# Two halves of an activation, one matmul of 512 columns: the first feed-forward product of a two-layer encoder

## The chip, the cores and the metric

The kernel runs on one core of a Trainium2 chip. The metric is the device time of one execution in microseconds (us), shown as the median of the runs of a kernel. TensorE is called PE here, its loading of a stationary operand PEld, VectorE DVE, ScalarE ACT, GpSimd POOL and SyncE SP.

## What is computed

The reference is a trunk of two layers over 256 tokens of width 1024. In each layer four token mixers are gated and summed, and then comes the feed-forward part, which the change touches:

```
def rms_norm(x, g):
    y = x * lax.rsqrt(jnp.mean(x * x, axis=-1, keepdims=True) + NORM_EPS)
    return y * g

def hybrid_layer(x, ...):
    ...
    x = x + jnp.sum(gates * proj, axis=2) @ w_o
    hf = rms_norm(x, g_ffn)
    x = x + jnp.square(jax.nn.relu(hf @ w_up)) @ w_down     # w_up 1024 x 4096, w_down 4096 x 1024
    return x
```

All data are fp32. One layer follows the other, and a last `rms_norm` closes the trunk.

## The kernel before, in words

**Products in halves.** PE is given operands of the type fp32r. Every fp32 operand is kept as two such tensors, a high half (its cast) and a low half (what the cast leaves over), and a product is the sum of three matmuls: high by high, high by low and low by high. The helper `mm3` (L122 to L124) issues them into one PSUM tile. The operand that is loaded into PE is the stationary one; the other one streams past it column by column. Each matmul brings its own load of the stationary operand, also where two matmuls in a row use the same one.

**Weights.** `weights` (L103) fetches a 128 x 1024 tile by a DMA issued on SP (L110), casts it to the high half `hi` on ACT (L114) and takes the rest `lo` on DVE (L115). There are 5 buffers for `raw` and 4 each for `hi` and `lo`, so the cast of a tile waits until PE has let go of the tile four before it.

**The first product.** `w_up` comes in 32 tiles of 128 hidden units. For one tile, `mtile` runs over the 8 blocks `k` of the model width: stationary is the block of the weight, and the 256 columns (tokens) of the activation `xg2` move past it, so 24 matmuls of 256 columns fill half of a PSUM tile `pu` of 512 columns. The high and the low half of `xg2` are two tiles, `xgh` and `xgl`, which `scale_split` writes on ACT (L293) and DVE (L294).

**On the way out of PSUM.** `hidden` (L797) makes the squared ReLU and its two halves:

```
nc.scalar.activation(r, ps[:, :T], AF.Relu)                                            # L801
nc.vector.scalar_tensor_tensor(t, ps[:, :T], 0.0, r, op0=ALU.max, op1=ALU.mult)        # L802
nc.scalar.copy(hi, t)                                                                  # L803, into U
nc.vector.tensor_tensor(lo, t, hi, op=ALU.subtract)                                    # L804, into U
```

**The second product.** `second` takes one hidden tile as the stationary operand and lets 512 columns of `w_dn` move past it: 12 matmuls of 512 columns for a tile, into four PSUM tiles `pd` that gather over all 32 hidden tiles.

**The order of the work.** The order on PE is that of the program. For the other engines a scheduler sets the order when the kernel is built, and an engine keeps to it at run time: an instruction that waits holds up all that stand behind it. In the loop over `i`, a step is the first product of tile `i` followed by the second product of tile `i - 2` (`LAG` is 2). It begins with a block of three tiles (`EARLY`): their first four `k`, the transposes of the other half of the activation, their last four `k`, and then at once the second product of tile 0, which needs `hidden` of tile 0. From `i = 3` on the loop runs in pairs, 29 steps to a layer.

Of the kernel before, what the change touches and what calls it, by code (L numbers as in the profile page):

```python
# [15 lines left out]
F32R = mybir.dt.float32r  # L19
I32 = mybir.dt.int32  # L20
AF = mybir.ActivationFunctionType
ALU = mybir.AluOpType
AX = mybir.AxisListType.X

P = 128
T = 256
D = 1024
KT = D // P
# [42 lines left out]
def hybrid_trunk(ctx: ExitStack, tc: tile.TileContext, xT, xtok, pos, small, gfin, abias, w_lat, w_v, w_in, w_uq, w_ukv,  # L71
                 w_gate, w_br, w_o, w_up, w_dn, out):
    nc = tc.nc
# [5 lines left out]
    act = ctx.enter_context(tc.tile_pool(name="act", bufs=1))  # L79
# [10 lines left out]
    def nm(s):  # L90
        count[0] += 1
        return f"{s}_{count[0]}"
# [9 lines left out]
    def weights(src, n=WCOLS, pieces=1, between=None):  # L102
        raw = rawp.tile([P, WCOLS], F32, tag="raw", name=nm("raw"))  # L103
        hi = whp.tile([P, WCOLS], F32R, tag="hi", name=nm("hi"))
        lo = wlp.tile([P, WCOLS], F32R, tag="lo", name=nm("lo"))
        share[0] += 1
        eng = nc.gpsimd if share[1] and share[0] % share[1] == 0 else nc.vector
        w = n // pieces
        for c in range(0, n, w):
            nc.sync.dma_start(raw[:, c:c + w], src[:, c:c + w])  # L110
            if c == 0 and between is not None:
                between()
        for c in range(0, n, w):
            cut = nc.scalar.copy(hi[:, c:c + w], raw[:, c:c + w])  # L114
            done = eng.tensor_tensor(lo[:, c:c + w], raw[:, c:c + w], hi[:, c:c + w], op=ALU.subtract)  # L115
        if eng is nc.vector:
            share[2] = done
        return hi, lo, done, cut

    def mm3(ps, stat, mov, first, last, late_mov=False):  # L120
        (sh, sl), (mh, ml) = stat[:2], mov[:2]
        nc.tensor.matmul(ps, sh, mh, start=first, stop=False)  # L122
        nc.tensor.matmul(ps, *((sl, mh) if late_mov else (sh, ml)), start=False, stop=False)  # L123
        nc.tensor.matmul(ps, *((sh, ml) if late_mov else (sl, mh)), start=False, stop=last)  # L124

    def cols(pair, i):
        return pair[0][:, i * P:(i + 1) * P], pair[1][:, i * P:(i + 1) * P]

    def part(pair, i):
        return pair[0][:, i, :], pair[1][:, i, :]  # L130
# [151 lines left out]
        return rb  # L282

    def new_xg():
        return (act.tile([P, KT, T], F32R, tag="xgh", name=nm("xgh")),
                act.tile([P, KT, T], F32R, tag="xgl", name=nm("xgl")))

    def scale_split(xg, k, src, g, on_vector=False):

# [6 lines left out]
    def to_features(half, dst, gcol, pool, tag):  # L296

        for pr in range(2):
            pt = pool.tile([P, 512], F32, tag=tag, name=nm("pt"))
            for j in range(2):  # L300
                k = 4 * half + 2 * pr + j
                for b in range(NB):
                    nc.tensor.transpose(pt[:, j * T + b * P:j * T + (b + 1) * P], X[:, b, k * P:(k + 1) * P], ident)
            for j in range(2):
                k = 4 * half + 2 * pr + j
                scale_split(dst, k, pt[:, j * T:(j + 1) * T], gcol(k))
# [9 lines left out]
    for _ in range(WARM):  # L316
        nc.tensor.matmul(warm[:, 0:P], o256, o256, start=True, stop=True)

    xg = new_xg()
    acc2 = tmp.tile([P, 2, T], F32, tag="d1", name="acc2", bufs=1)  # L320
    total = acc2[:, 0, :]
# [3 lines left out]
    for l in range(L):  # L325
# [7 lines left out]
        def tick():  # L333
            if side:
                for f in side.pop(0):
                    f()
# [4 lines left out]
        def mtile(ps, src, rhs, pieces=1):  # L341
            w = weights(src, pieces=pieces)
            for k in range(KT):
                mm3(ps, cols(w, k), part(rhs, k), k == 0, k == KT - 1)
            tick()
# [4 lines left out]
        for g in range(KT // 2):  # L350
            def stream(k0, k1):
                nc.sync.dma_start(xin[:, k0:k1, :], xT[:, k0:k1, :])
                for k in range(k0, k1):
                    scale_split(xg, k, xin[:, k, :], col(C_GMIX + k), on_vector=k % 2 == 1)

            if l == 0 and g == 0:
                stream(0, 1)
                w = weights(w_lat[l, g], 2 * LAT, pieces=2, between=lambda: stream(1, 2))
            else:
                if l == 0:  # L360
                    stream(2 * g, 2 * g + 2)
                w = weights(w_lat[l, g], 2 * LAT, pieces=1 if l else 2)
# [4 lines left out]
            for j in range(2):  # L367
                k, o = 2 * g + j, j * LAT
# [40 lines left out]
        for b in range(NB):  # L409
            nc.vector.scalar_tensor_tensor(z[:, b, :], plat[b][:, 384:388], rc[:, b:b + 1], s[:, C_BF:C_BF + HEADS],  # L410
                                           op0=ALU.mult, op1=ALU.add)
# [240 lines left out]
        def mla():  # L652
            w = weights(w_uq[l])
            for pr in range(2):
                ps = new_ps("puq")
                for e in range(2):
                    h = 2 * pr + e
                    for k in range(2):
                        mm3(ps[:, e * T:(e + 1) * T], cols(w, 2 * h + k), part(lat, k), k == 0, k == 1)
                nc.vector.tensor_tensor(qB[:, 2 * pr:2 * pr + 2, :], ps2(ps), CS, op=ALU.mult)  # L660
            w = weights(w_ukv[l], 512)
            for pr in range(2):
                ps = new_ps("puk")
                mm3(ps[:, :T], cols(w, pr), part(lat, 2), True, True)
                nc.scalar.copy(kB[0:64, 2 * pr, :], ps[0:64, :T])
                nc.scalar.copy(kB[64:P, 2 * pr + 1, :], ps[64:P, :T])
            ps = new_ps("puv")
            for b in range(NB):
                st = (lat[0][:, 2, b * P:(b + 1) * P], lat[1][:, 2, b * P:(b + 1) * P])
                mm3(ps[:, b * 256:(b + 1) * 256], st, (w[0][:, 256:512], w[1][:, 256:512]), True, True)  # L670
            nc.scalar.copy(VB.rearrange("p b d -> p (b d)"), ps)
            tick()
# [92 lines left out]
        def block(pair, k, b):  # L765
            return pair[0][:, k, b * P:(b + 1) * P], pair[1][:, k, b * P:(b + 1) * P]

        xg2 = new_xg()
        po = {(b, h): new_ps("po") for h in range(2) for b in range(NB)}

# [8 lines left out]
        for kp, h in ((0, 0), (0, 1), (1, 0), (1, 1), (2, 0), (2, 1), (3, 0), (3, 1)):  # L779
            w = weights(w_o[l, kp, h])  # L780
            for b in range(NB):
                for j in range(2):
                    k = 2 * kp + j
# [13 lines left out]
        def hidden(i, ps):  # L797
            t = tmp.tile([P, T], F32, tag="ut", name=nm("ut"))
            r = tmp.tile([P, T], F32, tag="sq", name=nm("ur"))
            hi, lo = U[:, i % RING, 0, :], U[:, i % RING, 1, :]  # L800
            nc.scalar.activation(r, ps[:, :T], AF.Relu)  # L801
            nc.vector.scalar_tensor_tensor(t, ps[:, :T], 0.0, r, op0=ALU.max, op1=ALU.mult)  # L802
            nc.scalar.copy(hi, t)  # L803
            nc.vector.tensor_tensor(lo, t, hi, op=ALU.subtract)  # L804

        def new_pu(i):
            pool, tag = ((psc, "sc"), (ppv, "pv"), (pms, "ms"), (pms, "ms"))[i % 4]
            return pool.tile([P, 512], F32, tag=tag, name=nm("pu"))

        EARLY = 3  # L810
        ws = [weights(w_up[l, i]) for i in range(EARLY)]
        pu = [new_pu(i) for i in range(EARLY)]
        for half in range(2):
            for i in range(EARLY):
                for k in range(4 * half, 4 * half + 4):
                    mm3(pu[i][:, :T], cols(ws[i], k), part(xg2, k), k == 0, k == KT - 1)
                if half == 0 and i == 0:
                    to_features(1, xg2, gffn, pmm, "mm")
        for i in range(EARLY):
            hidden(i, pu[i])  # L820
        pd = {(b, h): new_ps("pd") for b in range(NB) for h in range(2)}

        def second(i, w, b, h):
            st = U[:, i % RING, 0, b * P:(b + 1) * P], U[:, i % RING, 1, b * P:(b + 1) * P]
            tokens(pd[b, h], st, w, h, i == 0, i == FT - 1)
# [5 lines left out]
        last = []  # L831
        for i in range(FT + LAG):
            if EARLY <= i < FT:
                ps = new_pu(i)
                mtile(ps[:, :T], w_up[l, i], xg2)
                hidden(i, ps)
            d = i - LAG
            if d < 0:
                continue
            w = weights(w_dn[l, d])  # L840
            if d >= FT - 2:
                last.append((d, w))
                continue
            for b in range(NB):
                for h in range(2):
                    second(d, w, b, h)

        if l + 1 < L:
            xg = new_xg()
            s1 = sm[l + 1]  # L850

            def gmix(k):
                return s1[:, C_GMIX + k:C_GMIX + k + 1]

            for h in range(2):
                for b in range(NB):
                    for d, w in last:
                        second(d, w, b, h)
                    added(b, h)
                    if (h, b) == (1, 0):  # L860
                        to_features(0, xg, gmix, pms, "ms")
            stream_turn.append(lambda xg=xg, gmix=gmix: to_features(1, xg, gmix, pms, "ms"))
            continue
# [99 lines left out]
```

## Time and profile before

| what | value |
|---|---|
| runs | 844.81 us median (844.4 to 846.23, 3 runs) |
| the profiled execution, its own time | 843.17 us |
| its span in the trace | 841.4 us |
| PE busy | 823.5 us, 98% of the span |
| PEld busy | 757.9 us, 90% |
| DVE busy | 570.1 us, 68% |
| ACT busy | 449.5 us, 53% |
| POOL busy | 153.0 us, 18% |
| mean granted share of PE's clock | 0.998 |

The span reaches from the first to the last instruction of the program; the execution's own time is 1.8 us longer. Busy times of the engines overlap. The end of a matmul in the trace is a model, and matmuls overlap in it, so what one costs is read from the distance between the starts of two that follow each other, not from its duration.

### The profile page before, as it was taken

Reading aid. Unit: us, or ns where it says so; the run is one execution under the profiler, and the core shown is the slowest. Engines: PE = TensorE matmul, PEld = TensorE weight load, DVE = VectorE, ACT = ScalarE, POOL = GpSimd, SP = SyncE. Lnnn points to the kernel's source line nnn. Section 1 sums busy time; section 2 is a strip of 40 time slices with the busy share of each in tenths; the row PEclk is TensorE's granted clock in tenths of the full one; section 3 lists DMA queues with packets and bytes.
Section 4 is the critical chain, followed back from the end, with each engine's and each line's share of the span. In section 5 each row is a group of like instructions: output and inputs, shape, how many; then the busy total and the mean of one; then the engine's idle time right before and its main releaser. Section 6 shows DMA issues by size and latency. Waiting matters only on the chain.

```text
span 841.4 us, 14516 instructions
## 1 busy us (share of the span) xinstructions
PE 823.5 (98%) x5646; PEld 757.9 (90%) x5646; DVE 570.1 (68%) x948; ACT 449.5 (53%) x757; POOL 153.0 (18%) x156
## 2 busy tenths in 40 slices
PE   8999999999999999999999999999999999999996
PEld 7879999999889999999899899999998899999995
DVE  7899984787675555555578899557866655555554
ACT  6755546654464444444485664485445554545443
POOL 6534232133200000000014332312331000000000
PEclk9999999999999999999999999999999999999999
DMA  8765343455556555656554534345555555555531
GB/s 278 223 211 173 125 140 128 160 184 192 161 165 201 179 196 181 193 181 197 165 174 160 190 129 149 130 133 173 193 176 200 174 183 194 188 189 181 194 127 50
DMA packets 42549, 145.55 MB, mean 173 GB/s; under 512 B 5104, under 2 KB 7408, under 8 KB 42352
## 3 DMA queue, kind: packets, MB, share of 16 engines
q1 hardware_dynamic: 41904, 142.98, 52.7%
q10 hardware_dynamic: 576, 1.64, 0.6%
q8 instruction: 44, 0.72, 0.4%
q14 instruction: 25, 0.20, 0.1%
HBM read 143.55 MB, written 1.05 MB: 172 GB/s over the span
## 4 chain that ended last, share of the span: by engine, by line
PE 91%; DVE 5%; issue 2%; POOL 1%; DMA 1%; ACT 0%; SPq 0%; POOLq 0%; DVEq 0%; ACTq 0%
PE pgt L122 7%; PE pgt L123 7%; PE pgt L124 7%; PE pu L123 7%; PE pu L124 7%; PE pd L123 7%; PE pu L122 7%; PE pd L122 7%; PE pd L124 7%; PE S L555 2%; DVE lo L115 2%; PE pqk L122 2%; PE pPV L593 2%; PE pqk L123 2%; PE pqk L124 2%; PE po L122 2%
## 5 line engine op out<-in xcount | busy, mean ns | idle before, releaser
L115 DVE TENSOR_TENSOR lo<-raw,hi 128x1024 fp32r<-128x1024 f32 (+3 forms) x241 | 298.4, 1241 | 196.6 <-ACT hi L114 194.4
L114 ACT CAST hi<-raw 128x1024 fp32r<-128x1024 f32 (+2 forms) x273 | 278.4, 1024 | 266.9 <-issue 208.7
L122 PE MATMUL pgt<-xgh,hi 128*128 128x256 f32 x512 | 149.5, 292 | 0.0
L122 PE MATMUL pu<-xgh,hi 128*128 128x256 f32 x512 | 144.9, 283 | 0.7 <-ACT xgh L293 0.7
L123 PE MATMUL pu<-xgl,hi 128*128 128x256 f32 x512 | 145.1, 283 | 0.3
L124 PE MATMUL pu<-xgh,lo 128*128 128x256 f32 x512 | 144.9, 283 | 0.0
L123 PE MATMUL pgt<-xgl,hi 128*128 128x256 f32 x512 | 144.7, 283 | 0.0
L124 PE MATMUL pgt<-xgh,lo 128*128 128x256 f32 x512 | 144.7, 283 | 0.0
L123 PE MATMUL pd<-hi,u 128*128 128x512 f32 x256 | 100.5, 393 | 1.1 <-DVE u L804 1.1
L122 PEld LDWEIGHTS pu<-xgh,hi 128*128 128x128 f32 x512 | 98.0, 191 | 3.4 <-ACT xgh L293 1.1
L122 PE MATMUL pd<-hi,u 128*128 128x512 f32 x256 | 100.7, 393 | 0.4 <-ACT u L803 0.4
L123 PEld LDWEIGHTS pu<-xgl,hi 128*128 128x128 f32 x512 | 98.0, 191 | 3.0 <-DVE xgl L294 0.7
L124 PE MATMUL pd<-lo,u 128*128 128x512 f32 x256 | 99.6, 389 | 0.0
L122 PEld LDWEIGHTS pgt<-xgh,hi 128*128 128x128 f32 x512 | 97.9, 191 | 0.8 <-issue 0.3
L123 PEld LDWEIGHTS pgt<-xgl,hi 128*128 128x128 f32 x512 | 98.1, 192 | 0.4
L124 PEld LDWEIGHTS pu<-xgh,lo 128*128 128x128 f32 x512 | 98.0, 191 | 0.0
L124 PEld LDWEIGHTS pgt<-xgh,lo 128*128 128x128 f32 x512 | 97.9, 191 | 0.0
L115 POOL TENSOR_TENSOR lo<-raw,hi 128x1024 fp32r<-128x1024 f32 (+1 forms) x32 | 77.2, 2414 | 110.7 <-ACT hi L114 106.1
L491 DVE SCALAR_TENSOR_TENSOR cacc<-up,sm,cacc 128x256 f32<-128x256 f32 x120 | 77.4, 689 | 0.0
L124 PEld LDWEIGHTS pd<-lo,u 128*128 128x128 f32 x256 | 48.1, 188 | 10.4
L123 PEld LDWEIGHTS pd<-hi,u 128*128 128x128 f32 x256 | 48.3, 189 | 9.4 <-DVE u L804 1.7
L122 PEld LDWEIGHTS pd<-hi,u 128*128 128x128 f32 x256 | 48.3, 189 | 9.2 <-ACT u L803 0.8
(254 smaller groups left out, 1356.8 us busy)
## 6 DMA issues: line engine op xcount, KB each, us to landing
raw<-in_w_gate SPq DMA_DIRECT2D x64, 512.0 KB, 3.8
raw<-in_w_up SPq DMA_DIRECT2D x64, 512.0 KB, 4.1
raw<-in_w_dn SPq DMA_DIRECT2D x64, 512.0 KB, 3.9
raw<-in_w_in SPq DMA_DIRECT2D x23, 512.0 KB, 4.2
raw<-in_w_br SPq DMA_DIRECT2D x16, 512.0 KB, 3.6
raw<-in_w_o SPq DMA_DIRECT2D x16, 512.0 KB, 4.4
raw<-in_w_v SPq DMA_DIRECT2D x8, 512.0 KB, 4.3
raw<-in_w_lat SPq DMA_DIRECT2D x8, 210.0 KB, 4.9
```

Source lines behind the costliest of these rows:

```text
L114: cut = nc.scalar.copy(hi[:, c:c + w], raw[:, c:c + w])
L115: done = eng.tensor_tensor(lo[:, c:c + w], raw[:, c:c + w], hi[:, c:c + w], op=ALU.subtract)
L122: nc.tensor.matmul(ps, sh, mh, start=first, stop=False)
L123: nc.tensor.matmul(ps, *((sl, mh) if late_mov else (sh, ml)), start=False, stop=False)
L124: nc.tensor.matmul(ps, *((sh, ml) if late_mov else (sl, mh)), start=False, stop=last)
L491: ins = nc.vector.scalar_tensor_tensor(cacc[:, c, :], up[:, c, j:j + T], wcol, cacc[:, c, :], op0=ALU.mult, op1=ALU.add)
L555: nc.tensor.matmul(sl, q[:, b * P:(b + 1) * P], k[:, 0:n], start=True, stop=True)
L593: nc.tensor.matmul(po[o:o + 64, 0:T], v[:, 0, vo:vo + HD], pts[:, 0:T], start=True, stop=False)
```

## The change

The two halves of the activation become one tile `xg` of shape 128 x 8 x 2 x 256, in which the high and the low half of a block `k` lie side by side. `mm2` replaces `mm3` in the first product: one matmul moves all 512 columns (high and low half) past the high half of the weight, and a second one moves the 256 columns of the high half past the low half of the weight, onto the left half of the PSUM tile. The PSUM tile then holds two partial sums side by side, and `hidden` adds them: ACT copies the right half out, DVE adds the left half to it, and a second DVE instruction makes the squared ReLU from the sum. The other users of the activation see the same two views as before.

```
+    def mm2(ps, stat, mov, first, last):
+        (sh, sl), (mh, both) = stat[:2], mov
+        nc.tensor.matmul(ps, sh, both, start=first, stop=False)
+        nc.tensor.matmul(ps[:, 0:T], sl, mh, start=False, stop=last)
+    def both(three, i):
+        return three[0][:, i, :], three[2][:, i, :, :]
...
     def new_xg():
-        return (act.tile([P, KT, T], F32R, tag="xgh", name=nm("xgh")),
-                act.tile([P, KT, T], F32R, tag="xgl", name=nm("xgl")))
+        xg = act.tile([P, KT, 2, T], F32R, tag="xg", name=nm("xg"))
+        return xg[:, :, 0, :], xg[:, :, 1, :], xg
...
             hi, lo = U[:, i % RING, 0, :], U[:, i % RING, 1, :]
-            nc.scalar.activation(r, ps[:, :T], AF.Relu)
-            nc.vector.scalar_tensor_tensor(t, ps[:, :T], 0.0, r, op0=ALU.max, op1=ALU.mult)
+            nc.scalar.copy(t, ps[:, T:512])
+            nc.vector.tensor_tensor(r, ps[:, :T], t, op=ALU.add)
+            nc.vector.scalar_tensor_tensor(t, r, 0.0, r, op0=ALU.max, op1=ALU.mult)
             nc.scalar.copy(hi, t)
             nc.vector.tensor_tensor(lo, t, hi, op=ALU.subtract)
...
-                    mm3(pu[i][:, :T], cols(ws[i], k), part(xg2, k), k == 0, k == KT - 1)
+                    mm2(pu[i], cols(ws[i], k), both(xg2, k), k == 0, k == KT - 1)
...
-                mtile(ps[:, :T], w_up[l, i], xg2)
+                w = weights(w_up[l, i])
+                for k in range(KT):
+                    mm2(ps, cols(w, k), both(xg2, k), k == 0, k == KT - 1)
                 hidden(i, ps)
```

What the engines are given differs in these places and in no other. On PE, at the beginning of the first product of a layer (`pu` the PSUM tile, `hi` and `lo` the halves of the weight), it was:

```order
L122 MATMUL pu_2905<-xgh_2705,hi_2888 128x256
L123 MATMUL pu_2905<-xgl_2706,hi_2888 128x256
L124 MATMUL pu_2905<-xgh_2705,lo_2889 128x256
L122 MATMUL pu_2905<-xgh_2705,hi_2888 128x256
L123 MATMUL pu_2905<-xgl_2706,hi_2888 128x256
L124 MATMUL pu_2905<-xgh_2705,lo_2889 128x256
```

and it is now:

```order
L131 MATMUL pu_2903<-xg_2704,hi_2886 128x512
L132 MATMUL pu_2903<-xg_2704,lo_2887 128x256
L131 MATMUL pu_2903<-xg_2704,hi_2886 128x512
L132 MATMUL pu_2903<-xg_2704,lo_2887 128x256
L131 MATMUL pu_2903<-xg_2704,hi_2886 128x512
```

Of three matmuls two have become one of 512 columns; the 256 columns of L124 (now L132) stay. Over both layers 1024 matmuls of 256 columns with their 1024 weight loads give way to 512 of 512 columns with 512 loads.

On ACT, at the end of the block of three tiles of layer 0 (`hi` a cast of a weight, `ur` or `ut` what is read from `pu`, `u` the high half of a hidden tile), it was:

```order
L114 CAST hi_3040<-raw_3039 128x1024
L801 ACTIVATE ur_2999<-pu_2905 128x256
L114 CAST hi_3076<-raw_3075 128x1024
L801 ACTIVATE ur_3005<-pu_2906 128x256
L803 CAST u_2886<-ut_2998 128x256
L114 CAST hi_3095<-raw_3094 128x1024
L801 ACTIVATE ur_3011<-pu_2907 128x256
```

and it is now:

```order
L115 CAST hi_3017<-raw_3016 128x1024
L812 COPY ut_2972<-pu_2903 128x256
L115 CAST hi_3046<-raw_3045 128x1024
L812 COPY ut_2979<-pu_2904 128x256
L115 CAST hi_3065<-raw_3064 128x1024
L815 CAST u_2884<-ut_2972 128x256
L812 COPY ut_2986<-pu_2905 128x256
```

The cast `u` of hidden tile 0 has moved from the fifth place to the sixth, behind the third cast of a weight.

On DVE at the same place (`lo` the low half of a weight, `u` the low half of a hidden tile), it was:

```order
L115 TENSOR_TENSOR lo_3041<-raw_3039,hi_3040 128x1024
L802 SCALAR_TENSOR_TENSOR ut_2998<-pu_2905,ur_2999 128x256
L115 TENSOR_TENSOR lo_3077<-raw_3075,hi_3076 128x1024
L804 TENSOR_TENSOR u_2886<-ut_2998,u_2886 128x256
L802 SCALAR_TENSOR_TENSOR ut_3004<-pu_2906,ur_3005 128x256
```

and it is now:

```order
L116 TENSOR_TENSOR lo_3018<-raw_3016,hi_3017 128x1024
L813 TENSOR_TENSOR ur_2973<-pu_2903,ut_2972 128x256
L116 TENSOR_TENSOR lo_3047<-raw_3045,hi_3046 128x1024
L814 SCALAR_TENSOR_TENSOR ut_2972<-ur_2973 128x256
L813 TENSOR_TENSOR ur_2980<-pu_2904,ut_2979 128x256
L116 TENSOR_TENSOR lo_3066<-raw_3064,hi_3065 128x1024
L816 TENSOR_TENSOR u_2884<-ut_2972,u_2884 128x256
```

Between the first `lo` and the low half `u` of hidden tile 0 stood two instructions, and now stand five: the square `ut` of tile 0, which is an instruction of its own now, the sum `ur` of tile 1, and a third `lo`. Layer 1 has the same order. In the 29 steps the two orders are alike but for the one added DVE instruction, right behind the sum.

## Rows read from the trace of the kernel before

**Rows 1.** The page, part 4: the chain that ended last, by engine.
```profile
PE 91%; DVE 5%; issue 2%; POOL 1%; DMA 1%; ACT 0%; SPq 0%; POOLq 0%; DVEq 0%; ACTq 0%
```

**Rows 2.** Busy time by windows, 27 steps: us, each engine (instructions), PEclk, DMA share, GB/s.
```profile
256.90:408.60 151.70, 151.70 (x974) 138.46 (x973) 84.27 (x108) 72.48 (x108) 0.00 (x0) 1.00 0.58 186
```

**Rows 3.** Timeline of PE, one step: start, us, line, operation, tiles, shapes.
```profile
341.21 0.40 PE L122 MATMUL pd<-hi,u 128*128 128x512 f32 x1
341.45 0.40 PE L123 MATMUL pd<-hi,u 128*128 128x512 f32 x1
...
342.60 0.39 PE L122 MATMUL pd<-hi,u 128*128 128x512 f32 x1
...
343.96 0.28 PE L122 MATMUL pu<-xgh,hi 128*128 128x256 f32 x1
344.07 0.28 PE L123 MATMUL pu<-xgl,hi 128*128 128x256 f32 x1
...
344.31 0.28 PE L122 MATMUL pu<-xgh,hi 128*128 128x256 f32 x1
...
346.71 0.28 PE L124 MATMUL pu<-xgh,lo 128*128 128x256 f32 x1
346.83 0.40 PE L122 MATMUL pd<-hi,u 128*128 128x512 f32 x1
```

**Rows 4.** What touches the tile pu: weight loads of one line, min/median/max ns.
```profile
L123 PEld LDWEIGHTS pu<-xgl,hi x512: 186/192/193, 239.5 to 824.5; 128*128 128x128 f32 x171
```

**Rows 5.** Groups by shape, of DVE, then of ACT: busy us, mean ns, idle.
```profile
L802 DVE SCALAR_TENSOR_TENSOR ut<-pu,ur 128x256 f32<-128x256 f32 x64 | 26.5, 417 | 0.9 <-ACT ur L801 0.9
...
L598 DVE TENSOR_TENSOR brl<-pPV,brh 128x256 fp32r<-128x256 f32 x12 | 5.0, 420 | 1.3 <-ACT brh L597 1.0
...
L801 ACT ACTIVATE ur<-pu 128x256 f32<-128x256 f32 x64 | 24.2, 378 | 1.8 <-PE pu L124 1.8
...
L281 ACT COPY rb<-pb 128x256 f32<-128x256 f32 x4 | 1.5, 369 | 0.0
```

**Rows 6.** Timeline of PE, where layer 0 goes over to the second product.
```profile
249.89 0.28 PE L124 MATMUL pu<-xgh,lo 128*128 128x256 f32 x1
250.38 0.50 PE L122 MATMUL pd<-hi,u 128*128 128x512 f32 x1 [0.21 <-ACT u L803]
251.41 0.50 PE L123 MATMUL pd<-hi,u 128*128 128x512 f32 x1 [0.53 <-DVE u L804]
```

**Rows 7.** Timeline of ACT at the same place.
```profile
247.25 1.05 ACT L114 CAST hi<-raw 128x1024 fp32r<-128x1024 f32 x1 [2.06 <-PE pu L123]
...
248.69 1.05 ACT L114 CAST hi<-raw 128x1024 fp32r<-128x1024 f32 x1
...
249.92 0.41 ACT L803 CAST u<-ut 128x256 fp32r<-128x256 f32 x1
250.23 1.04 ACT L114 CAST hi<-raw 128x1024 fp32r<-128x1024 f32 x1
```

**Rows 8.** Timeline of DVE at the same place.
```profile
248.33 1.23 DVE L115 TENSOR_TENSOR lo<-raw,hi 128x1024 fp32r<-128x1024 f32 x1 [2.62 <-ACT hi L114]
249.47 0.41 DVE L802 SCALAR_TENSOR_TENSOR ut<-pu,ur 128x256 f32<-128x256 f32 x1
249.81 1.21 DVE L115 TENSOR_TENSOR lo<-raw,hi 128x1024 fp32r<-128x1024 f32 x1
250.94 0.42 DVE L804 TENSOR_TENSOR u<-ut,u 128x256 fp32r<-128x256 f32 x1
```

**Rows 9.** Timeline of PE at the same place in layer 1.
```profile
660.96 0.50 PE L122 MATMUL pd<-hi,u 128*128 128x512 f32 x1 [0.22 <-ACT u L803]
661.99 0.50 PE L123 MATMUL pd<-hi,u 128*128 128x512 f32 x1 [0.53 <-DVE u L804]
```

## The prediction

> **What bounds the kernel now.** First the chain that ended last: 91% of the span is PE [rows 1], so look for what sets PE's pace. Then the windows, over 27 steps of the feed-forward loop of layer 0: PE is busy for all of the 151.70 us, at the full granted clock of 1.00 (2.4 GHz), while DVE is busy for 84.27, which is 3.12 us of each step of 5.62, and ACT for 72.48 [rows 2]. In this loop nothing but PE counts, as long as the others keep up. Then the timeline of PE, where one step must be read by starts. It goes from 341.21 to 346.83, or 5.62 us: twelve `pd` matmuls of 512 columns up to 343.96 and then 24 `pu` matmuls of 256 columns. From 344.31 to 346.71 lie 20 of the latter, 2.40 us, or 120 ns each; from 342.60 to 343.96 lie six of the former, 1.36 us, or 226.7 ns each [rows 3]. The columns alone, one for each period of 2.4 GHz, would take 106.7 and 213.3 ns. Both leave **13.3 ns**: in this trace a matmul costs its columns and a fixed part that does not grow with them. That is what the change can earn, for it moves exactly as many columns as before (512 + 256 against 3 x 256), in fewer instructions.
>
> The last view is the place where a layer goes over from the block of three tiles to the second product. It is one of few in the feed-forward part where PE stands still: the last `pu` starts at 249.89, the first `pd` waits for the cast `u` on ACT until 250.38, the next for the low half `u` on DVE until 251.41 [rows 6]. Layer 1 has the same wait, 660.96 to 661.99 [rows 9].
>
> **Term 1: PE in the 29 steps.** A merge replaces two matmuls of 120 ns by one of 226.7: 240 - 226.7 = 13.3 ns. There are 32 tiles x 8 blocks x 2 layers = 512 merges; the 48 in the two blocks of three tiles run into the wait of rows 6 and are counted there. The other 464 earn 464 x 13.3 = **6.2 us**, all of it on the path.
>
> The trace has no stretch in which matmuls of 512 and 256 columns alternate, so this price needs bounds. The six `pd` from 341.21 to 342.60, right behind the 256-column stretch, take 231.7 ns each, and the first of them 240; the first `pu` behind the 512-column stretch takes 110 (343.96 to 344.07) [rows 3]. An alternating stream may look like either edge at every matmul. Upper end for the cost: 240 + 120 against 360, so a merge earns nothing. Lower end: 226.7 + 110, so it earns 23 ns, or 10.8 us in all. I take 13.3: the raised and the lowered edge have opposite signs and were read off the same transition, and the steady values stand between them.
>
> The 512 weight loads that go with the merged matmuls read 192 ns each [rows 4], but they run beside the matmuls and follow each other at the same 120 ns; their saving is already in the distance between starts. Nothing is added for them.
>
> **Term 2: the longer way out of PSUM.** In a step ACT swaps a ReLU of 378 ns for a copy, whose like takes 369. DVE swaps 417 ns for a sum from PSUM (420 for its nearest like) and a squaring that I put at the same 417, so it gains some 0.42 us of work [rows 5]. That makes 3.5 of 5.5 us on DVE. The result of a step is needed by PE only two steps later, some 11 us off, and PE waits for neither engine in the 151.70 us of rows 2. I cost it at nothing there. The longer hold on `pu` is covered too, since four such tiles rotate. If the cover went, PE would wait once a step for half a microsecond, 29 us in all.
>
> At the transition there is no cover. On DVE, 0.34 us separate a squaring from the `lo` behind it, and 1.13 to 1.14 us a `lo` from what comes next: 248.33, 249.47, 249.81, 250.94 [rows 8]. The changed order puts three more instructions ahead of the low half `u` of tile 0: its squaring (0.34), the sum of tile 1 (0.34) and a third `lo` (1.13), together **1.81 us**. Is that `lo` ready by then? Its cast on ACT needs PE to let go of the weight of the third tile. The casts at 247.25 and 248.69 are 1.44 apart, so the third may start at 250.13 and be done at about 251.2, ahead of DVE, which reaches it at 251.6; DVE is the limit. Before the block's end the merges have pulled PE, and with it the first cast and the whole chain, ahead by some 12 x 13.3 = 0.17 us. So the second `pd` starts not at 251.41 but 1.64 us later, at 253.05. The cast `u` of tile 0, now behind the third weight cast (250.23 and 249.92 in the trace of before [rows 7]), lets the first `pd` start at about 251.7, inside the same wait. Two layers: **3.3 us** lost. Bounds: 1.4 a layer if DVE closes its gaps, 2.0 if the third cast is late; 2.8 to 4.0.
>
> The queue of SP has the same order of DMAs as before, and POOL has no work in this stretch [rows 2]. The single tile for both halves makes the first matmul of a block wait for the low half, where the second one did before. Only the first blocks of a layer could feel it, and their matmul of the low half had to wait for the same write; I cost it at nothing, with 0.1 us a layer as the bound.
>
> **The sum.** -6.2 + 3.3 = **-2.9 us**. The span goes from 841.4 to 838.5, the profiled execution from 843.17 to 840.3. That execution lies 1.6 us under the median of the runs, and against the median of 844.81 the forecast is **841.9 us**. A difference under 0.2% (1.7 us) can't be told from none.
>
> **A rule that speaks against the change.** The fixed part of 13.3 ns is the trace's, from two widths [rows 3]. The Trainium skill, in "TensorE: Matmul & The Clock Gate", section "Back-to-back issue gap", gives the distance of two matmuls at the full clock as the columns over 2.4 GHz plus 2.5 ns. By that rule a merge would earn 2.5 ns and Term 1 would be 1.2 us. The trace disagrees at both widths: 120 ns where the rule gives 109, 226.7 where it gives 216.
>
> **The rivals.**
> - *Merges earn 8 ns.* Every 512 behind a 256 costs 231.7 as the six behind the stretch do, and the 256 stays at 120. Term 1 is 464 x 8.3 = 3.9 us, the sum -0.6, the time 844.2: no change. For it speaks that raised mean, against it the lowered 110.
> - *Merges earn nothing (slower).* Every 512 costs what the first behind the stretch does, 240. Term 1 is gone, Term 2 stays: +3.3, 848.1 us. The point from which this decides: a merge that earns under (3.3 - 1.7) / 464 = 3.4 ns, so a 512 of over 236.6 ns in the alternating stream. Against it: only the first two or so of a dozen are so long.
> - *Merges earn 23 ns.* The 256 behind each 512 costs 110 and the 512 stays at 226.7: -10.8 + 3.3 = -7.5, or 837.3. For it speaks the one row at 343.96.
> - *Only a fifth of the fixed part is saved*, 2.7 ns a merge, and the rest comes back with the added columns: 464 x 2.7 = 1.2 us, the sum +2.1, 846.9. Rows 3 speak against it at both widths. It is about what the rule above would give.
> - *The change doesn't lengthen the wait*, because the engines reach `u` sooner than the spacings of rows 7 and 8 say: -6.2, 838.6. The built order speaks against it.
>
> **How the numbers follow.** Forecast 0.52 (its own range 840.3 to 843.4, from 11 to 16 ns a merge and the bounds of Term 2), merges at 8 ns 0.18, at nothing 0.07, at 23 ns 0.15, at 2.7 ns 0.03, no longer wait 0.05. Faster by over 0.2% means under 843.1: 0.47 of the forecast, the 0.15, the 0.05 and 0.01 of the first rival make 0.68. Slower means over 846.5: 0.07 and 0.02 make 0.09. The rest, 0.23, is no change. The range 837.8 to 845.8 takes in the forecast and the first rival whole, the unchanged wait and a part of the 23 ns; outside stay the rest of that (0.09), the slower one (0.07) and 2.7 ns (0.03).
>
> **What the profile of the changed kernel would show.** Term 1: a step of 5.62 - 8 x 0.0133 = 5.51 us, in which a 512 and the 256 behind it take 347 ns from start to start of the next 512; PE still busy throughout, DVE at some 64%. Term 2: the second `pd` of a layer 1.6 us later against the end of the casts, behind a wait put down to `u` on DVE. I am wrong if the step stays at 5.6 (the alternating stream pays), if it falls below 5.47 (it earns more than the fixed part), if PE shows waits for ACT or DVE inside the steps, or if the wait at the transition has not grown.

## The result, and the profile after

| | before | after |
|---|---|---|
| median of the runs, us | 844.81 (842.87 to 846.23, 9 runs) | 849.51 (845.8 to 852.69, 9 runs) |
| the profiled execution, us | 843.17 | 848.35 |
| its span, us | 841.4 | 846.6 |
| its mean granted share of PE's clock | 0.998 | 0.996 |

The ratio is 1.0058, interval 1.0039 to 1.0076: **slower by 0.6%**. The forecast was 841.9 with a range of 837.8 to 845.8; slower had a chance of 0.09.

First the windows, over the same stretch of the loop as [rows 2]:

```profile
256.90:408.60 151.70, 151.70 (x761) 127.46 (x760) 95.37 (x135) 71.97 (x108) 0.00 (x0) 1.00 0.60 186
```

PE is still busy throughout at the full clock, and DVE at 95.37 / 151.70 = 63%. No engine has become a new bound in the steps. The timeline of PE over one step, as in [rows 3]:

```profile
344.26 0.40 PE L123 MATMUL pd<-hi,u 128*128 128x512 f32 x1
...
347.04 0.39 PE L131 MATMUL pu<-xg,hi 128*128 128x512 f32 x1
347.27 0.28 PE L132 MATMUL pu<-xg,lo 128*128 128x256 f32 x1
347.38 0.40 PE L131 MATMUL pu<-xg,hi 128*128 128x512 f32 x1
...
349.85 0.40 PE L123 MATMUL pd<-hi,u 128*128 128x512 f32 x1
```

From 344.26 to 349.85 are 5.59 us (5.593 over the 29 steps of a layer), where 5.51 were forecast. The eight pairs take 349.85 - 347.04 = 2.81 us, 351 ns each instead of 347, and the twelve `pd` take 2.78 us, where twelve at 226.7 would take 2.72. The step gives up 0.08 us of the 0.107 it should have gained.

Then the transition, as in [rows 6, 9]; PE in both layers:

```profile
253.56 0.49 PE L123 MATMUL pd<-hi,u 128*128 128x512 f32 x1 [1.75 <-ACT u L815]
254.92 0.50 PE L124 MATMUL pd<-hi,u 128*128 128x512 f32 x1 [0.87 <-DVE u L816]
...
666.59 0.50 PE L123 MATMUL pd<-hi,u 128*128 128x512 f32 x1 [1.75 <-ACT u L815]
667.96 0.50 PE L124 MATMUL pd<-hi,u 128*128 128x512 f32 x1 [0.86 <-DVE u L816]
```

The waits of 0.21 and 0.53 us have become 1.75 and 0.87. DVE shows why, as in [rows 8]:

```profile
250.04 1.23 DVE L116 TENSOR_TENSOR lo<-raw,hi 128x1024 fp32r<-128x1024 f32 x1 [2.52 <-ACT hi L115]
251.18 0.42 DVE L813 TENSOR_TENSOR ur<-pu,ut 128x256 f32<-128x256 f32 x1
251.51 1.22 DVE L116 TENSOR_TENSOR lo<-raw,hi 128x1024 fp32r<-128x1024 f32 x1
252.65 0.42 DVE L814 SCALAR_TENSOR_TENSOR ut<-ur 128x256 f32<-128x256 f32 x1
252.98 0.42 DVE L813 TENSOR_TENSOR ur<-pu,ut 128x256 f32<-128x256 f32 x1
253.32 1.21 DVE L116 TENSOR_TENSOR lo<-raw,hi 128x1024 fp32r<-128x1024 f32 x1
254.45 0.41 DVE L816 TENSOR_TENSOR u<-ut,u 128x256 fp32r<-128x256 f32 x1
```

From the first `lo` to the low half `u` it is now 4.41 us instead of 2.61: 1.80 more, for the three instructions that stand in between, end to end.

A third place had not been in the forecast, the end of layer 0:

```profile
420.98 0.50 PE L123 MATMUL pd<-hi,u 128*128 128x512 f32 x1 [0.38 <-ACT u L815]
422.08 0.50 PE L124 MATMUL pd<-hi,u 128*128 128x512 f32 x1 [0.60 <-DVE u L816]
```

There the last hidden tile of the layer, tile 31, goes into the second product, and PE had no wait before. ACT in the kernel before, and then ACT in the changed kernel, at this place (the weight of 840 columns belongs to layer 1):

```profile
416.73 0.41 ACT L803 CAST u<-ut 128x256 fp32r<-128x256 f32 x1 [1.15 <-DVE ut L802]
417.04 0.90 ACT L114 CAST hi<-raw 128x840 fp32r<-128x840 f32 x1
```

```profile
419.73 0.90 ACT L115 CAST hi<-raw 128x840 fp32r<-128x840 f32 x1 [1.46 <-PE pd L124]
420.53 0.40 ACT L815 CAST u<-ut 128x256 fp32r<-128x256 f32 x1
```

The cast `u` of tile 31 has moved behind a weight cast that must first wait 1.46 us for PE. The section on the change said that the orders differ in the places shown and in no other. That was wrong: here too the scheduler chose another order.

### The profile page after: what moved, and what is told of

It is laid out like the page before. It is cut to its first block, busy times and chain, and to the rows that moved or that the text cites. A ratio compares the mean times of both kernels' runs of the same rounds, so it can differ in the third digit from the quotient of the medians.

```text
span 846.6 us, 13552 instructions
## 1 busy us (share of the span) xinstructions
PE 822.4 (97%) x5134; PEld 730.3 (86%) x5134; DVE 596.1 (70%) x1012; ACT 449.8 (53%) x757; POOL 151.9 (18%) x156
## 3 DMA queue, kind: packets, MB, share of 16 engines
q10 hardware_dynamic: 576, 1.64, 0.6%
## 4 chain that ended last, share of the span: by engine, by line
PE 90%; DVE 5%; issue 2%; POOL 1%; DMA 1%; ACT 1%; SPq 0%; POOLq 0%; DVEq 0%
PE pu L131 14%; PE pgt L123 7%; PE pgt L124 7%; PE pgt L125 7%; PE pd L124 7%; PE pd L123 7%; PE pd L125 7%; PE pu L132 7%; PE S L566 2%; DVE lo L116 2%; PE pqk L123 2%; PE pPV L604 2%; PE pqk L124 2%; PE pqk L125 2%; PE po L123 2%
## 5 line engine op out<-in xcount | busy, mean ns | idle before, releaser
L131 PE MATMUL pu<-xg,hi 128*128 128x512 f32 x512 | 182.9, 397 | 1.8 <-DVE xg L305 1.8
L123 PE MATMUL pgt<-xg,hi 128*128 128x256 f32 x512 | 149.5, 292 | 0.0
L124 PE MATMUL pgt<-xg,hi 128*128 128x256 f32 x512 | 144.7, 283 | 0.0
L125 PE MATMUL pgt<-xg,lo 128*128 128x256 f32 x512 | 144.7, 283 | 0.0
L132 PE MATMUL pu<-xg,lo 128*128 128x256 f32 x512 | 143.5, 280 | 0.0
L131 PEld LDWEIGHTS pu<-xg,hi 128*128 128x128 f32 x512 | 96.2, 188 | 25.1 <-DVE xg L305 2.4
L124 PE MATMUL pd<-hi,u 128*128 128x512 f32 x256 | 100.4, 392 | 2.3 <-DVE u L816 2.3
L132 PEld LDWEIGHTS pu<-xg,lo 128*128 128x128 f32 x512 | 96.6, 189 | 2.3
L123 PEld LDWEIGHTS pgt<-xg,hi 128*128 128x128 f32 x512 | 97.9, 191 | 0.8 <-issue 0.3
L124 PEld LDWEIGHTS pgt<-xg,hi 128*128 128x128 f32 x512 | 98.1, 192 | 0.4
L125 PEld LDWEIGHTS pgt<-xg,lo 128*128 128x128 f32 x512 | 97.9, 191 | 0.0
L124 PEld LDWEIGHTS pd<-hi,u 128*128 128x128 f32 x256 | 48.2, 188 | 11.9 <-DVE u L816 3.3
L749 POOL TENSOR_TENSOR yt<-yt 128x512 f32<-128x512 f32 x16 | 26.2, 1640 | 105.2 <-DVE yt L748 93.7
L277 POOL TENSOR_TENSOR rc<-rv,misc 128x2 f32<-128x2 f32 x4 | 3.8, 945 | 218.6 <-DVE rv L272 209.7
```

The lines of the kernel that those rows point to most:

```text
L131: nc.tensor.matmul(ps, sh, both, start=first, stop=False)
L132: nc.tensor.matmul(ps[:, 0:T], sl, mh, start=False, stop=last)
L277: last_pow[0] = nc.gpsimd.tensor_tensor(rc, v, mhalf[:, :NB], op=ALU.pow)
L749: nc.gpsimd.tensor_tensor(yt[:, 0:2, :], yt[:, 0:2, :], yt[:, 2:4, :], op=ALU.add)
```

## The experiments

Against the first profile of before, 1.76 us of the 5.2 in the spans lay in the token mixer of layer 0, in code that the change doesn't touch. So the kernel before was profiled once more. Below, "512s" and "256s" are matmuls of 512 and of 256 columns, the transition is the place of [rows 6, 9], and the "mixer" is the token mixer of a layer.

**before_again.** No edit.

> The kernel before, profiled once more. The profiled pair differed by 1.76 us in the token mixer of layer 0, in code that the change does not touch: behind the wait for qkA the granted clock fell to one half for 3.4 us in the changed kernel and not in the one before. Theory 'chance': it is not the change's; of 23 runs of the kernel before, 20 had a mean granted clock of 0.996 or less, so most of them hold such a stretch. Expected: a mean clock of 0.996 or 0.994, a time of 844 to 846 us, and the half clock behind the wait for qkA at about 50 us. Theory 'change': the kernel before does not fall there; a mean clock of 0.998, a time near 842.5, a wait for qkA of 1.9 us.

Measured: 844.99 us, span 843.2, mean clock 0.996. PE in the mixer of layer 0, and the window in which the granted clock is low:

```profile
50.05 0.92 PE L555 MATMUL S<-qkA 64*128 64x128 f32 x4 [1.88 <-DVE qkA L636]
...
51.72 0.63 PE L123 MATMUL pv<-hi,xgl 128*128 128x512 f32 x1
52.15 0.63 PE L124 MATMUL pv<-lo,xgh 128*128 128x512 f32 x1
```

```profile
51.04:54.45 3.41, 3.41 (x10) 2.73 (x10) 3.41 (x11) 2.87 (x7) 0.00 (x0) 0.50 0.39 138
```

Behind the wait for `qkA` the granted clock is 0.50 (1.2 GHz) for 3.41 us, the matmuls of 512 columns stand 0.43 us apart instead of 0.227, and the stretch costs 1.6 us, just as in the changed kernel. So 'chance' holds for the half clock: the kernel before has it too, and its first profile was one of the few executions without it. The wait itself is 1.9 us here and 3.1 in the changed kernel. It varies within one program: `pairs` and `pairs_timed` below are the same kernel and show 3.3 and 1.9. But 3.1 to 3.4 us stand in nine of the eleven profiles with the new tile `xg` and in neither of the two of the kernel before, so whether the change makes the long wait likelier is not settled.

Against this execution the spans differ by 846.6 - 843.2 = 3.4 us, and the starts of matmuls at the same places in the two traces say where. The row of the block ends at the first `pu` behind the transposes, and the row of the transition goes from there to the second `pd`:

| stretch | after minus before, us |
|---|---|
| up to the first `pu` of layer 0 | 0.0 |
| block of three tiles to the transposes, both layers | +0.2 |
| transition, both layers (1.62 each) | +3.2 |
| 29 steps, both layers (0.80 and 0.81) | -1.6 |
| end of layer 0 | +1.6 |
| mixers of layer 1 | -0.1 |

The medians differ by 4.7, so more than 1 us is not in this pair of traces.

**after_again.** The changed kernel once more.

> The changed kernel once more. Both theories: some 848 to 850 us, steps of 5.59 us, the second pd matmul of each layer about 1.6 us later than before. Theory 'clock' (the longer waits let PE's clock fall to half in some executions): runs of over 850 us have a mean granted clock of 0.990 or less, runs under 848 one of 0.995 or more, and any stretch at half clock in the profile begins at the end of a wait of PE. Theory 'work alone': the times do not go with the granted clock.

Measured: 849.73 us (848.04 to 853.09, 6 runs) against 844.51, ratio 1.0073 [1.0053, 1.0093]. Its profile (850.4 us, clock 0.990) holds what the first lacked. Two windows behind the transition of layer 0, then PE there:

```profile
257.00:260.41 3.41, 3.41 (x10) 2.63 (x9) 0.85 (x3) 1.17 (x2) 0.00 (x0) 0.50 0.55 185
260.41:263.82 3.41, 3.41 (x20) 2.94 (x19) 1.23 (x1) 1.10 (x2) 0.00 (x0) 1.00 0.24 61
```

```profile
254.53 0.49 PE L123 MATMUL pd<-hi,u 128*128 128x512 f32 x1 [1.75 <-ACT u L815]
255.89 0.50 PE L124 MATMUL pd<-hi,u 128*128 128x512 f32 x1 [0.87 <-DVE u L816]
...
257.70 0.63 PE L124 MATMUL pd<-hi,u 128*128 128x512 f32 x1
258.13 0.63 PE L125 MATMUL pd<-lo,u 128*128 128x512 f32 x1
```

Ten matmuls fit in where the next 3.41 us hold twenty. It is so in both layers here and in neither layer of the first profile, with waits of the same length. Set against the first profile, matmul by matmul, the half clock costs 1.6 us in layer 0 and 1.4 in layer 1, where its first 0.5 us fell into the wait. (The 1.65 us a layer in the expectation of `fill` below is too much.) Of the other kernels with the long waits, `split` has it behind the transition of layer 1 alone and `grouped` behind neither; no profile with the waits of the kernel before has it there. Over the 9 first runs the time goes with the mean clock: 845.8 to 848.35 at 0.995 and 0.996, 851.17 to 852.69 at 0.989 and 0.990.

**split.** The new way out of PSUM without the merge.

```
-        nc.tensor.matmul(ps, sh, both, start=first, stop=False)
+        nc.tensor.matmul(ps[:, 0:T], sh, both[:, 0, :], start=first, stop=False)
+        nc.tensor.matmul(ps[:, T:512], sh, both[:, 1, :], start=False, stop=False)
```

> The 512-column matmul is taken apart into two of 256 columns that fill the two halves of the PSUM tile; way out of PSUM and order on ACT and DVE are those of the changed kernel. Theory 'mixed widths' (the steps earn little because 512 and 256 columns alternate): steps back at 5.62 us as before the change, waits at the transitions (+1.6 us a layer) and at the end of layer 0 (+1.6) as in the changed kernel, so +4.8 us to the kernel before, 849.6, plus what the clock takes. Theory 'way out' (the added DVE work slows PE in the steps): steps of about 5.70 us, +9.4 us, 854.

Measured: 851.5 us (850.05 to 853.26, 6 runs), ratio 1.009 [1.0074, 1.0106]. One step of it:

```profile
346.38 0.40 PE L123 MATMUL pd<-hi,u 128*128 128x512 f32 x1
...
352.00 0.40 PE L123 MATMUL pd<-hi,u 128*128 128x512 f32 x1
```

The step is 5.62 as before, without a wait inside it, and the transition has the waits of the changed kernel (1.68 and 0.86). So the DVE instruction added to the steps costs nothing, nor does changing between the halves of the PSUM tile and of the weight, which `split` does too, at equal widths. The merge as written does earn a little, 5.62 - 5.593 us a step; the medians, 849.73 against 851.5, go the same way, but the intervals of their ratios overlap.

**edges_old.** The first product and the way out of before for the three tiles of the block and tile 31, the change for the other 28 (below: the old edges).

```
-                    mm2(pu[i], cols(ws[i], k), both(xg2, k), k == 0, k == KT - 1)
+                    mm3(pu[i][:, :T], cols(ws[i], k), part(xg2, k), k == 0, k == KT - 1)
...
+            if i < EARLY or i == FT - 1:
+                nc.scalar.activation(r, ps[:, :T], AF.Relu)
+                nc.vector.scalar_tensor_tensor(t, ps[:, :T], 0.0, r, op0=ALU.max, op1=ALU.mult)
+            else:
...
```

> Tiles 0 to 2 and tile 31 of each layer keep three matmuls and the old way out; the other 28 are merged. Order on ACT and DVE at the transitions and at the layer's end as before the change. Both theories of the steps: 5.59 us a step, no added wait, so -1.5 us to the kernel before, 843.3. Theory 'clock': granted clock and spread of the runs as in the kernel before (0.997 or more in most). If the waits were not what costs, the time stays near that of the changed kernel, 849.

Measured: 844.41 us (841.1 to 845.05, 12 runs), ratio 0.9996 [0.9983, 1.0008]. The first `pd` waits 0.22 us again, and the end of layer 0 has no wait. Undoing four tiles of 32 takes the whole loss back. The steps are as dear as in the changed kernel, 5.593; their 56 x 0.026 = 1.5 us are not seen in the median. The clock that was expected, 0.997 or more in most runs, did not come: it is 0.993 in 8 of the 12, at 844.2 to 845.1 us, and 0.995 to 0.997 in the other four, at 841.1 to 843.4. The profile, one of the eight, spends 6.83 us at half clock in the mixer of layer 0 where before_again has 3.41, and comes to the first `pu` 1.0 us later.

**grouped.** The changed kernel, but in a step all eight 512s of a tile come first, and then its eight 256s.

```
                 for k in range(KT):
-                    mm2(ps, cols(w, k), both(xg2, k), k == 0, k == KT - 1)
+                    nc.tensor.matmul(ps, cols(w, k)[0], both(xg2, k)[1], start=k == 0, stop=False)
+                for k in range(KT):
+                    nc.tensor.matmul(ps[:, 0:T], cols(w, k)[1], both(xg2, k)[0], start=False, stop=k == KT - 1)
```

> In the steps all eight 512-column matmuls of a tile come first, then the eight of 256 columns; all else as in the changed kernel (the cast of the last hidden tile of layer 0 stands in its old place again). Theory 'mixed widths': a step is 12 + 8 matmuls at 226.7 ns, 8 at 120 and one transition of 20 ns, 5.51 us, so -6.2 us in the steps and +3.3 at the transitions, 842. Theory 'way out' or 'the merged matmul itself costs more than 227 ns': steps of 5.59 us, and some 846 to 847.

One step of it:

```profile
342.87 0.40 PE L123 MATMUL pd<-hi,u 128*128 128x512 f32 x1
...
345.62 1.98 PE L849 MATMUL pu<-xg,hi 128*128 128x512 f32 x8
347.43 1.11 PE L851 MATMUL pu<-xg,lo 128*128 128x256 f32 x8
348.38 0.40 PE L123 MATMUL pd<-hi,u 128*128 128x512 f32 x1
```

The step is 5.51 us, what Term 1 had said: the same matmuls earn their 13.3 ns when equal widths stand together. The order of the casts at the end of layer 0 is the old one in this build, and nothing is lost there; the transition still waits 1.75 and 0.86. The profiled span is 840.3, 2.9 under that of before_again, which is the sum of the forecast. But the median is 844.28 (842.04 to 846.38, 12 runs), ratio 1.0 [0.9987, 1.0014]: at a mean clock of 0.996 the runs take 842.0 and 842.4, and at 0.988 and 0.989 some 845.3 to 846.4.

**grouped_edges.** The old edges of `edges_old` and the steps of `grouped` together.

> Both mends together: in 28 steps a layer the eight matmuls of 512 columns come first and then the eight of 256, and the three tiles of the block and the last tile of a layer keep the three matmuls and the way out of PSUM of the kernel before. Theory 'mixed widths' with 'way out': a step takes 5.51 us, 0.107 less than before, so 56 x 0.107 = 6.0 us are gained; the second pd of a layer starts with the wait of the kernel before (0.5 us and less), and nothing is lost at the end of layer 0. Time 844.5 - 6.0 = 838.5, ratio 0.993 (0.991 to 0.995), faster than both kernels. Theory 'clock alone': the gain of the steps is eaten by stretches at half clock wherever they fall, as the 844.3 of the grouped kernel seemed to say; ratio 0.998 to 1.000.

Measured: 839.07 us (838.73 to 840.94, 5 runs) against 844.43, ratio 0.9939 [0.9923, 0.9955]; the step is 5.51. From its table of waits, and then from that of the changed kernel (us in all, times, the longest):

```profile
PE pd L124 <- DVE u L820: 1.1, 2, 0.5
```

```profile
PE pd L124 <- DVE u L816: 2.3, 3, 0.9
```

With the waits of the kernel before, the mean clock stays at 0.994 to 0.996, as in the 9 runs of before beside it, and the gain of the steps arrives: 5.4 us of 6.0. To `grouped` it is 844.28 - 839.07 = 5.2 us, more than the 3.4 that the block and the transition cost in the table, as the lower clocks of `grouped` let expect.

**pairs** and **pairs_timed.** Two 512s and two 256s in turn, with the old edges.

```
+                for kk in range(0, 0 if i == FT - 1 else KT, 2):
+                    for k in (kk, kk + 1):
+                        nc.tensor.matmul(ps, cols(w, k)[0], both(xg2, k)[1], start=k == 0, stop=False)
+                    for k in (kk, kk + 1):
+                        nc.tensor.matmul(ps[:, 0:T], cols(w, k)[1], both(xg2, k)[0], start=False, stop=k == KT - 1)
```

> As the kernel with the old edges, but in 28 steps a layer two matmuls of 512 columns are followed by two of 256, four times. The orders of ACT and DVE stay. Alternating one by one made a step of 5.594 us, eight and eight made 5.513; steady prices (226.7 and 120) would make 5.494. Theory 'price per return': each return from 256 to 512 columns costs some 12 ns, spread over the 512s behind it: eight returns 0.10, one 0.02, four 0.05: a step of 5.54 us. Theory 'only one by one': the dear rhythm needs a change of width at every matmul; 5.51 us. Theory 'any mixing within the tile': as dear as alternating, 5.59 us.

> The kernel with two matmuls of 512 columns and two of 256 in turn once more, now timed: the step measured 5.507 us, 0.113 less than before, so 56 x 0.113 = 6.3 us less than before where the edges of the block cost nothing: 844.5 - 6.3 = 838.2, ratio 0.9925 (0.990 to 0.995). If the edges or the clock take part of it, as in the grouped kernel: ratio 0.996 or more.

PE in `pairs_timed`:

```profile
348.87 0.62 PE L856 MATMUL pu<-xg,hi 128*128 128x512 f32 x2
349.32 0.40 PE L858 MATMUL pu<-xg,lo 128*128 128x256 f32 x2
349.56 0.63 PE L856 MATMUL pu<-xg,hi 128*128 128x512 f32 x2
```

A group of four takes 349.56 - 348.87 = 0.69 us, two steady pairs, and the step 5.507. 'Only one by one' holds, a price per return doesn't. Times: 838.49 in the one run of the first, and 838.95 (836.86 to 839.91, 6 runs) against 844.55, ratio 0.9932 [0.9912, 0.9951]. **This beats both kernels**, level with grouped_edges.

**pair_then_ones.** The first two pairs of a tile grouped, the other six one by one, with the old edges. In the block of three tiles of the changed kernel the alternating stream had run at the steady price (four pairs in 1.38 us):

```profile
245.75 0.40 PE L131 MATMUL pu<-xg,hi 128*128 128x512 f32 x1
245.98 0.28 PE L132 MATMUL pu<-xg,lo 128*128 128x256 f32 x1
...
247.13 0.40 PE L131 MATMUL pu<-xg,hi 128*128 128x512 f32 x1
```

> The kernel with the old edges, but in 28 steps a layer the first two 512s come together and then two 256s, and the other six pairs alternate one by one. In the block of three tiles of the changed kernel, behind transposes of 128 columns, the alternating stream had paid 346 ns a pair, the steady price, while in the steps, right behind the 512s of the second product, it paid 351 and left the next 512s dearer. Theory 'the start decides': begun behind two 256s the stream falls into the cheap rhythm of the block; 346 to 347 ns a pair and a step of 5.51 to 5.52 us. Theory 'alternation pays': each pair costs some 351 to 353 and the raised 512s behind stay; a step of 5.57 us or more.

```profile
346.35 0.40 PE L857 MATMUL pu<-xg,hi 128*128 128x512 f32 x1
346.58 0.28 PE L859 MATMUL pu<-xg,lo 128*128 128x256 f32 x1
...
348.47 0.40 PE L123 MATMUL pd<-hi,u 128*128 128x512 f32 x1
```

Six pairs in 2.12 us: 353 ns each, as 'alternation pays' had it. The step is 5.553 us, under that theory's 5.57 and well over the 5.52 of the other; the time of the one run 842.2. Beginning behind two 256s is not what makes the block's stream cheap. What does stays open. There is one more case of it: in after_again the step of layer 1 right behind the half clock.

```profile
674.46 0.40 PE L131 MATMUL pu<-xg,hi 128*128 128x512 f32 x1
...
677.24 0.40 PE L123 MATMUL pd<-hi,u 128*128 128x512 f32 x1
...
679.97 0.39 PE L131 MATMUL pu<-xg,hi 128*128 128x512 f32 x1
```

Eight pairs one by one take 2.78 us there, 347 ns each, and the step 5.51, where every other full step at the full clock in that execution has the same matmuls at 5.59. So the price is not fixed by the order of the matmuls alone. The `pd` just ahead were still raised (231, 236 and 228 ns), where the other steps of layer 1 begin behind `pd` at 226.7; no run tests whether that decides.

**fill** and **fill_half.** The changed kernel with matmuls that nobody reads in the wait of the transition, 22 and then 11.

```
+        fill = pms.tile([P, 512], F32, tag="ms", name=nm("fill"))
+        for _ in range(22):
+            nc.tensor.matmul(fill[:, 0:P], o256, o256, start=True, stop=True)
```

> The changed kernel with 22 matmuls of 128 columns put ahead of the first pd of a layer; they write a free PSUM tile that nobody reads, and the orders of ACT and DVE stay as they are. PE is busy for about 2.3 us of the wait and the waits end when they did, set by ACT and DVE. Theory 'clock': part of the loss is the half clock that follows the wait (4 us at 0.43 us a matmul of 512 in the second profile of the changed kernel, 1.65 us in each layer). With the fill the matmuls behind the second pd run 0.227 apart in both layers, no half clock stands in the records after 60 us, and the median goes from 849.7 to about 847.5 (ratio 1.0035 to 1.005). Theory 'wait alone': the wait is the whole loss and the clock falls or stays by chance; the median stays at 849 to 850 (ratio 1.006 to 1.007), with half clock behind the transition as often as before.

```profile
251.81 5.07 PE L835 MATMUL fill<-o 128*128 128x128 f32 x44
256.64 0.48 PE L123 MATMUL pd<-hi,u 128*128 128x512 f32 x1
```

The 22 stand in the trace as 44 and took 4.8 us; they delayed the first `pd` themselves. Measured 852.08 us (849.97 to 852.76, 5 runs), with the clock at 0.994 to 0.997. As a test of the wait it failed, so the number was halved.

> The kernel with the filled wait, with half the fill. A matmul of 128 columns on these fp32 data turned out to be two in the trace, so 22 of them kept PE for 4.8 us, not 2.3, and delayed the first pd from 253.6 to 256.6; that run could not show what the wait without half clock costs. With 11, PE is busy to about 254.2, the first pd starts there and the second at 254.9, as in the changed kernel. Theory 'clock': the half clock behind the transitions is gone from every execution, the mean clock is 0.994 to 0.997 as with 22 (0.989 to 0.996 in the changed kernel), and the median falls from 849.7 to 848 or less, with no value above 850. Theory 'wait alone': the median stays at 849 to 850 with values up to 853.

```profile
251.04 2.62 PE L835 MATMUL fill<-o 128*128 128x128 f32 x22
253.41 0.48 PE L123 MATMUL pd<-hi,u 128*128 128x512 f32 x1
254.32 0.50 PE L124 MATMUL pd<-hi,u 128*128 128x512 f32 x1 [0.43 <-DVE u L816]
254.66 0.40 PE L125 MATMUL pd<-lo,u 128*128 128x512 f32 x1
254.90 0.40 PE L123 MATMUL pd<-hi,u 128*128 128x512 f32 x1
```

The second `pd` starts as far behind the last `pu` (250.92) as in the changed kernel: 3.40 us. The median is 848.09 (847.53 to 849.8, 6 runs) against 844.55, ratio 1.0043 [1.0026, 1.0059], with clocks of 0.994 to 0.996 where after_again had 0.989 to 0.995. What is left is 3.5 us, the 3.4 of the table. So of the 5.2 us by which after_again was slower, about 1.7 are half clock behind the lengthened waits: time lost though PE worked. The size is rough, for the intervals of the two ratios overlap; but the runs of the changed kernel at 0.995 and more, without any fill, took 845.8 to 848.35 us, about as long as `fill_half`.

## Why the prediction was wrong

- **Term 2, the longer way out: right.** 1.64 us a layer were forecast, 1.62 came in each. DVE closed no gap and was the limit; the first `pd` waits for ACT inside the same delay, as said. The bound of 0.1 us a layer for the first blocks was reached and not passed (+0.2 for both layers).
- **Term 1, the merges: mis-sized.** Forecast 6.2 us, 13.3 ns a merge; it was 1.6, or 1.6 / 464 = 3.5 ns, beside the 3.4 ns from which the slower rival was to decide. Its own sign of being wrong, a step that stays at 5.6, came. The failing step is the choice between the bounds of the alternating stream: "the raised and the lowered edge have opposite signs and were read off the same transition, and the steady values stand between them". In the stream the edges don't cancel: a 512 behind a 256 costs up to 241 ns, a 256 behind a 512 takes 113 to 120, and the `pd` behind the stretch are raised for ten matmuls, not six. (The 240 and 110 that served as bounds were differences of starts given to 0.01 us; over the steps of the trace of before the first 512 takes 234 and the first 256 takes 113.) The 13.3 ns as such was right: the grouped and the paired step have it. The rule of the Trainium skill that was weighed there ("TensorE: Matmul & The Clock Gate", "Back-to-back issue gap"), which the section gives for an isolated matmul, came near in its sum, an estimate of 1.2 us against 1.6, but not for its own reason: with equal widths together the same merges earned 6.2.
- **Overlooked: the end of layer 0, +1.6 us.** The prediction took the orders to differ at the transition and by one DVE instruction a step, and had no term for this place. `grouped`, whose build has the cast of tile 31 in its old place, loses nothing there.
- **Overlooked: the clock, about 1.7 us.** Term 2 was priced as idle time alone. The granted clock falls to half behind the longer waits in some executions, and the matmuls that follow pay once more. The Trainium skill, on the same page, tells of another kernel in which frequent short idle times of PE between groups of matmuls made the clock go to and fro ("A second HAM failure mode: psum-queue depth-cycling"). The window at 257.00 is like it in so far as the clock fell behind short waits, 1.75 and 0.87 us; but there are only these two to a transition, and in the first profile they were not enough.
- **Costed at nothing, rightly:** the added DVE work in the steps (5.62 in `split`), and the weight loads (the step of `grouped` comes out at 5.51 without a term for them). SP's queue was not tested by itself; PE shows no wait in the steps.

Sum as it should have been: -1.6 + 3.2 + 0.2 + 1.6 + about 1.7 = +5.1, against 4.7 measured at first and 5.2 beside after_again.

## What to carry to other kernels

In the steps here fewer, wider matmuls earned their fixed cost when equal widths stood together: two and two was enough, one by one lost most of it. When a change lengthens a chain between engines, list every place where that chain has no cover, at each layer's beginning and end, and give those places the old code; four tiles of 32 decided the sign. A wait of PE can cost more than its length, through the clock behind it: here about 1.7 us on top of 3.4 for the waits of the block and the transition and 1.6 for those at the end of layer 0.

## What the runs showed of the hardware

- Alternating 512 and 256 columns one by one behind 512s: 351 to 353 ns a pair, against 226.7 + 120 = 346.7 steady and 0.69 us for two and two; the following 512s are raised to as much as 241 ns before they come back to 226.7. The same alternation took 346 in the block of three tiles, and 347 in one step of after_again. Which condition chooses between the two rhythms is not settled.
- The granted clock fell to 0.50 for 3.41 or 6.83 us at waits of 1.9 to 3.4 us in the mixer, and for 3.41 us behind the two of 1.75 and 0.87, in some executions and not in others of the same program. A stretch of 3.41 us cost 1.6 us where all of it fell on matmuls (before_again, layer 0 of after_again), and 1.4 where a part fell into the wait.
- A matmul of 128 columns on plain fp32 operands stood in the trace as two, of 0.11 us each.
